# Layer 1 of a two-layer decoder trunk: spacing of the side tasks between the matmuls of the main stream

## The chip, the cores and the metric

The kernel runs on one core of one Trainium2 chip. A core has five engines with a queue each, which run at the same time and wait for one another by semaphores: PE (TensorE, matrix products, written to PSUM), DVE (VectorE, elementwise work), ACT (ScalarE, functions of one operand, copies and rounding), POOL (GpSimd, elementwise work), and SP (SyncE, which here only issues DMAs). Each engine takes its instructions strictly in the order of the program. The metric is the device time of one execution in microseconds (us).

## The reference

Input is x (512 tokens by 2048 channels) and a condition c. There are two layers, each an RMS norm with scale and shift from c, a branch, a SiLU gate and a gated residual add. Layer 0 is attention with 32 heads of 64. Layer 1, which the change is about, is RWKV-7 time mixing:

```python
xx = shift(h) - h                       # token shift
xr, xw, xk, xv, xa, xg = (h + xx * mu[i] for i in range(6))
r, k, v, z = xr @ w_in[0], xk @ w_in[1], xv @ w_in[2], xg @ w_in[3]
decay = exp(-exp(-softplus(-(w0 + tanh(xw @ w1) @ w2)) - 0.5))
v = v + (v_first - v) * sigmoid(v0 + (xv @ v1) @ v2)
a = sigmoid(a0 + (xa @ a1) @ a2)
kk = normalised(k * k_k);  k = k * (1 + (a - 1) * k_a)
# per head, state S (64 x 64), for every token in turn:
S = S * w_t + (S @ -kk_t) outer (kk_t * a_t) + v_t outer k_t
y_t = S @ r_t
# layer norm of y per head, bonus (r . k * r_k) v, then (y * silu(z)) @ w_out
```

Every product of the wide projections is computed as three single-pass products of a high and a low part (`hi*whi + hi*wlo + lo*whi`), so each weight and each operand is split into two parts first.

## The kernel before, in words

The activations lie with channels on the 128 partitions and the 512 tokens in the free dimension, so a 2048-channel operand is 16 tiles `[128, 512]`. A projection to 128 output channels is one bank of PSUM (`pj`) into which 16 x 3 = 48 matmuls of 128x512 accumulate. These matmuls form the **main stream** (`backbone`): in layer 1 ten tiles of k (six more are computed with the norm), then 16 each of r, v, z and the output projection. For each four k-steps a weight block is loaded (`raw`, three buffers), rounded by ACT (`whi`) and completed by DVE (`wlo = raw - whi`).

All else of layer 1 is written as **side tasks**, Python generators that record their instructions between the matmuls of the main stream. The order of every engine's queue is the order of recording; nothing is reordered afterwards. A planner, the class `Flow`, decides when a task goes on. It has a time `fl.t`, which each recorded matmul advances by its length at one column per 1/2400 us, so by 0.213 for a 128x512 matmul and 0.64 for a k-step of three. A task that yields d is resumed once `fl.t` has advanced by d. A number behind a `yield` is thus an amount of PE work that is put between two steps of a task, and nothing else; no wait is in it, and the semaphores still decide when an instruction runs.

The side tasks of layer 1, in order of time:

- `lora_k`, one for each of the 16 channel tiles, 4.4 apart: the token-shift mixes of three operands (`m`), their rounding (`mh`, on ACT) and rests (`ml`), and 9 matmuls into three banks (`S`, `S`, `y`). The rest of the first operand is made by POOL, those of the other two by DVE.
- `lora_up`, 48 of them: 2 or 3 matmuls each and a sigmoid on ACT (`sig`), loop in `side`.
- `keys`, one per channel tile, `KEY` apart: norms, decays and the matrices `at`, `bk`, `gab` of the recurrence. It has a call of `means`: ACT rounds a tile (`mhi`), DVE makes the rest (`mlo`), and PE multiplies both by a block matrix for a mean over each head.
- `invert` and `inverse`: inverses of small triangular matrices by 30 steps of two elementwise operations (`lt`, `lane`) for each of four groups, on POOL for the first three, on DVE for the last (`DG`), where `DINV` is the planner time over which they are spread. `inverse` comes `INV` after its keys.
- `stage`: for each of 16 pairs of chunks (a chunk is 64 tokens of 8 heads) the loads `rt`, `bk`, `prk`, and for each chunk `L`, `QP`, `SV`, two halves of each; then `products` and `bonus`.
- `recur`: 32 chunks in turn, three **hops** each. A hop is a group of small matmuls that needs what DVE copied out of PSUM after the hop before (`xs`, `SV`); `hop()` holds it until `fl.t` enters the next multiple of `HOP`. After each pair `normed` does the layer norm, with two calls of `means`; a token `B` keeps `bonus` and `normed` from using `means` together.
- `gated` and `output`: the gate, and the last projection.

SP's queue carries all loads and stores of both, in the recorded order.

Of the kernel before, what the change touches and what calls it, by code (L numbers as in the profile page):

```python
# [131 lines left out]
def body(ctx, tc, a, out, dbg=None, stop=0):  # L132
# [260 lines left out]
    with ExitStack() as s0:  # L393
# [7 lines left out]
        with tc.tile_pool(name="st0", bufs=2, reuse_waits="tile") as q:  # L401
# [96 lines left out]
            cb, cs, i = silu_c(cbp)  # L498
# [11 lines left out]
            for i in range(4):  # L510
                o = bank("tr")
# [79 lines left out]
        fl = Flow()  # L591
# [5 lines left out]
        q = sq0.enter_context(tc.tile_pool(name="at", bufs=2, reuse_waits="tile"))  # L597
# [445 lines left out]
    fl = Flow()  # L1043
# [7 lines left out]
    q = pools.enter_context(tc.tile_pool(name="kq", bufs=2, reuse_waits="tile"))  # L1051
# [36 lines left out]
    def means(q, w, x, th, tl):  # L1088
        hi = q.tile([P, T], R, tag=th, name="mhi")
        lo = q.tile([P, T], R, tag=tl, name="mlo")  # L1090
        act_hi(hi, x)
        yield 0.6
        dve.tensor_tensor(out=lo, in0=x, in1=hi, op=OP.subtract)
        yield 1.8
        n = yield from need("S")
        ss = bank("S")
        pe.matmul(ss, w, hi, start=True, stop=False)
        pe.matmul(ss, w, lo, start=False, stop=True)
        return ss, n
# [34 lines left out]
    lspan = ((0, LW), (LW, LW + LA_), (NL - P, NL))  # L1134
    lb, la = [], []

    def lora_k(q, k):
        if k == 0:
            lb.extend(bank(t) for t in "SSy")
        hp = load(mq, h1d[k], "hp", (P, T + 1), bufs=NHP)  # L1140
        raw = load(q, a["lora"][k], "rawl", (P, NL))
        yield 4
        wh = q.tile([P, 1, NL], R, tag="whl", name="whl")
        wl = q.tile([P, 1, NL], R, tag="wll", name="wll")
        act_hi(wh[:, 0], raw)
        ns = (1, 4, 3)
        ms = [q.tile([P, T], F, tag=f"m{n}", name="m", bufs=1 + (n == 3)) for n in ns]
        d = q.tile([P, T], F, tag="d", name="d")
        pool.tensor_tensor(out=d, in0=hp[:, 0:T], in1=hp[:, 1:], op=OP.subtract)
        ts = [tuple(q.tile([P, T], R, tag=f"m{x}{n}", name="m" + x) for x in "hl") for n in ns]  # L1150
        yield 1.4
        for i in range(5):
            if i == 1:
                dve.tensor_tensor(out=wl[:, 0], in0=raw, in1=wh[:, 0], op=OP.subtract)
            if i < 3:
                dve.scalar_tensor_tensor(out=ms[i], in0=d,
                                         scalar=vecs[:, V_MU + ns[i], k:k + 1],
                                         in1=hp[:, 1:], op0=OP.mult, op1=OP.add)
            if 1 <= i < 4:
                act_hi(ts[i - 1][0], ms[i - 1])  # L1160
            if 2 <= i:
                e = pool if i - 2 < 1 else dve
                e.tensor_tensor(out=ts[i - 2][1], in0=ms[i - 2], in1=ts[i - 2][0],
                                op=OP.subtract)
            yield 0.7
        yield 1
        sp.dma_start(mxd[0, k], ms[2])
        premixed.add((0, k))
        for t, o, (m0, m1) in zip(ts, lb, lspan):
            mm3(o[0:m1 - m0, :], (wh, wl), 0, t, k == 0, k == KT - 1, m0, m1)  # L1170
            yield 1
        if k == KT - 1:
            lb.append(None)
# [294 lines left out]
    def stage(q, g, u):  # L1468

        rt = q.tile([P, NJ, UC, C], F, tag="rt", name="rt", bufs=2)  # L1470
        sp.dma_start(rt.rearrange("p j c t -> p j (c t)"), rTd[g][:, u])
        bk = q.tile([P, NJ, UC, 2, C], F, tag="bk", name="bk", bufs=2)
        yield 1
        for i in range(2):
            for h in range(2):
                sp.dma_start(bk.rearrange("p j c i t -> p (j c) i t")[HS[h], :, i, :],
                             bkd[g][HS[h], u, i ^ h].rearrange("p j (c t) -> p (j c) t", c=UC))
            yield 0.6
        yield from take("prk")
        prk = q.tile([P, NJ, UC, C], F, tag="prk", name="prk", bufs=2)  # L1480
        sp.dma_start(prk.rearrange("p j c t -> p j (c t)"), ipd[g][:, u])
        yield STW
        eI = q.tile([P, NJ, UC, C], F, tag="eI", name="eI", bufs=2)
        act.activation(eI, prk, AF.Exp, scale=-EDEC)
        yield 1
        dec = q.tile([P, NJ, UC], F, tag="dec", name="dec", bufs=3)
        pool.tensor_copy(dec, eI[:, :, :, C - 1])
        dve.tensor_tensor(out=rt, in0=rt, in1=eI, op=OP.mult)
        yield 1
        for j in range(NJ):  # L1490
            for h in range(2):
                s = HS[h]
                dve.scalar_tensor_tensor(out=prk[s, j], in0=rt[s, j],
                                         scalar=vecs[s, V_RK, NJ * g + j:NJ * g + j + 1],
                                         in1=bk[s, j, :, 1 - h, :], op0=OP.mult, op1=OP.mult)
            yield 0.6
        while any(NJ * g + i not in vd for i in range(NJ)):
            yield 0.2
        for c in range(UC):
            yield from take("chunk")  # L1500
            m = NCH * g + UC * u + c
            L, SV = ([q.tile([P, NJ] + w, F, tag=f"{m}{h}", name=f"{m}{h}", bufs=4)
                      for h in range(2)] for m, w in (("L", [2, C]), ("SV", [C])))
            svs[m] = SV
            qp = QP[m % 4]
            for h in range(2):
                s, t = HS[h], OS[h]
                sp.dma_start(L[h][s, :, 0, :], atd[g][s, u, :, c * C:c * C + C])
                dve.tensor_copy(L[h][s, :, 1, :], rt[s, :, c])
                sp.dma_start(qp[h][s], qtd[NJ * g:NJ * g + NJ, 64 * c:64 * c + 64,  # L1510
                                           4 * h + u, :].rearrange("j p t -> p j t"))
                sp.dma_start(SV[h][t], vtd[g][(UC * u + c) * C:(UC * u + c + 1) * C, h])
                if u == c == 0:
                    pool.memset(SV[h][s], 0.0)
                yield 0.6
            fl.start(fl.t + STW, products(q, m, c, L, SV, qp, bk, eI, dec))
            yield 2
        fl.start(fl.t + 2, bonus(q, g, u, prk))

    def products(q, m, c, L, SV, qp, bk, eI, dec):  # L1520
# [55 lines left out]
    def hop():  # L1576
        n = fl.t // HOP
        while fl.t // HOP == n:
# [163 lines left out]


    STW = 5
    DG, DINV = (3,), 25
    HOP = 3.9
    INV, KEY = 54, 9.8

    def side(q):
        for j, o in enumerate(ks):  # L1750
# [8 lines left out]
        q = pools.enter_context(tc.tile_pool(name="uq", bufs=2, reuse_waits="tile"))  # L1759
# [8 lines left out]
        for j in range(KT):  # L1768
            for n in range(3):
                if j % 4 == 0 and j < KT - 4:  # L1770
                    fl.start(fl.t, lora_w(q, j // 4 + 1, n))
                fl.start(fl.t, lora_up(q, j, n))
                yield 0.8
        while len(ups) < 3 * KT:
            yield 0.2
        yield 3
# [75 lines left out]
```

## Time and profile before

| | |
|---|---|
| median of 3 runs | 2428.52 us (2423.59 to 2431.46) |
| the profiled execution, its own time | 2426.4 us |
| its span, first to last instruction | 2424.7 us |
| PE busy | 2312.1 us (95%), 13626 matmuls |
| DVE / ACT / POOL busy | 1607.0 / 1254.5 / 701.4 us |
| mean granted clock of PE | 0.984 |

The stages of layer 1 in the trace, in us from the start of the span: `lora_k` 1203 to 1297, `lora_up` to 1355, `keys` to 1606, the inversion on DVE to 1646, the last inverses to 1695, first staging to 1750, recurrence to 2190, and the rest of the main stream to the end.

How to read it: all recording goes through one helper, so each row says L90, and the names of the tiles (out<-in) tell the places apart. In a list of waits a row reads: engine and output, what it waited for, microseconds in total, number of waits, the longest. `PEclk` is the clock of PE that was granted, as a share of full speed. PE's matmuls overlap in the records, so the start-to-start distance tells its pace, not the duration of one.

### The profile page before, as it was taken

How to read it: one execution, taken by the hardware profiler on the slowest of the kernel's cores; microseconds unless marked ns; L12 is line 12 of the kernel's file. 1: busy time of each engine (PE TensorE's matmuls, PEld its weight loads, DVE VectorE, ACT ScalarE, POOL GpSimd, SP SyncE). 2: the span in 40 equal slices, each digit the busy share in tenths (PEclk: the TensorE clock that was granted, in tenths of full speed). 3: DMA queues.
4: the chain of work that ended last, by engine and by line, in shares of the span. 5: the costliest groups of instructions: out<-in, count | busy, mean ns of one | idle time of the engine just before them, and what ended most of it. 6: DMA issues, size and time to landing. Idle time of an engine off the chain costs nothing. (4 is left out here: it accounts for less than half of the span.)

```text
span 2424.7 us, 39355 instructions
## 1 busy us (share of the span) xinstructions
PE 2312.1 (95%) x13626; PEld 1806.3 (74%) x13626; DVE 1607.0 (66%) x2850; ACT 1254.5 (52%) x2298; POOL 701.4 (29%) x1114
## 2 busy tenths in 40 slices
PE   6998999999999999998999999989899989999999
PEld 4786677878777778886766766777677767777887
DVE  6887878788788545336797667675477777655322
ACT  4425655555555544225646777754354556665221
POOL 0002424434323110110141218851264445440000
PEclk8999999999999999999999999999999999999999
DMA  8865566666665265445756999877776776635443
GB/s 303 327 230 183 184 197 209 203 207 219 199 210 183 88 201 185 146 135 153 230 169 210 296 283 264 262 220 204 206 197 178 194 187 190 180 121 178 153 139 95
DMA packets 388150, 480.20 MB, mean 198 GB/s; under 512 B 146032, under 2 KB 217840, under 8 KB 384112
## 3 DMA queue, kind: packets, MB, share of 16 engines
q1 hardware_dynamic: 386288, 475.08, 63.5%
q0 software_dynamic: 1664, 2.63, 0.3%
q8 instruction: 107, 1.75, 0.3%
q14 instruction: 91, 0.75, 0.1%
HBM read 381.63 MB, written 95.95 MB: 197 GB/s over the span
## 5 line engine op out<-in xcount | busy, mean ns | idle before, releaser
L90 PE MATMUL pj<-hi,whi 128*128 128x512 f32 x2416 | 986.6, 408 | 11.9 <-ACT hi L90 8.2
L90 PE MATMUL pj<-hi,wlo 128*128 128x512 f32 x2416 | 958.9, 397 | 5.9 <-DVE wlo L90 5.9
L90 PE MATMUL pj<-lo,whi 128*128 128x512 f32 x2416 | 959.8, 397 | 0.0
L90 DVE TENSOR_TENSOR wlo<-raw,whi 128x512 fp32r<-128x512 f32 (+2 forms) x628 | 474.4, 762 | 281.7 <-ACT whi L90 279.3
L90 ACT ACTIVATE whi<-raw 128x512 fp32r<-128x512 f32 (+2 forms) x628 | 394.2, 634 | 418.7 <-PE pj L90 220.1
L90 PEld LDWEIGHTS pj<-hi,whi 128*128 128x128 f32 x2416 | 459.2, 190 | 117.2 <-ACT hi L90 9.0
L90 PEld LDWEIGHTS pj<-lo,whi 128*128 128x128 f32 x2416 | 458.0, 190 | 108.9 <-DVE lo L90 0.6
L90 PEld LDWEIGHTS pj<-hi,wlo 128*128 128x128 f32 x2416 | 459.6, 190 | 100.4 <-DVE wlo L90 7.4
L90 DVE CUSTOM_DVE_ANT_0 wm<-wm,cb 128x1024 f32<-128x1024 f32 x128 | 157.6, 1231 | 0.3
L90 POOL TENSOR_SCALAR SV<-SV,dec 64x64 f32<-64x64 f32 x224 | 98.3, 461 | 113.5 <-DVE SV L90 71.5
L90 ACT ACTIVATE pr<-Sm,mx 128x128 f32<-128x128 f32 (+3 forms) x128 | 71.6, 559 | 89.2 <-POOL mx L90 89.0
L90 POOL TENSOR_SCALAR mx<-mx 128x1 f32<-128x1 f32 x128 | 66.3, 518 | 160.4 <-DVE mx L90 111.3
L90 POOL TENSOR_SCALAR pr<-pr,rc 128x128 f32<-128x128 f32 (+3 forms) x128 | 94.8, 741 | 28.4 <-DVE rc L90 20.1
L90 DVE CUSTOM_DVE_ANT_0 Sm<-S,cmask 128x128 f32<-128x128 f32 (+3 forms) x128 | 62.0, 485 | 36.9 <-PE S L90 36.1
L90 POOL TENSOR_TENSOR lt<-lane 128x30 f32<-128x30 f32 (+14 forms) x90 | 62.4, 693 | 65.1 <-DMA lane<-mld 58.3
L90 POOL TENSOR_TENSOR lane<-lane,lt 128x30 f32<-128x30 f32 (+14 forms) x90 | 65.1, 723 | 7.1
L90 POOL TENSOR_TENSOR bk<-bk,eI 128x512 f32<-128x512 f32 x32 | 36.4, 1137 | 105.9 <-PE S L90 90.1
L90 PE MATMUL S<-k,q 128*128 128x128 f32 (+7 forms) x256 | 62.5, 325 | 0.0
L90 POOL TENSOR_TENSOR acc<-acc,sq 128x512 f32<-128x512 f32 x14 | 18.1, 1295 | 150.7 <-ACT sq L90 150.7
L90 PE MATMUL tr<-ident,pr 128*128 128x128 f32 x320 | 56.8, 276 | 4.4 <-DVE rc L90 1.6
L90 PEld LDWEIGHTS tr<-ident,pr 128*128 128x128 f32 x320 | 41.4, 141 | 25.1 <-ACT pT L90 7.6
L90 DVE SCALAR_TENSOR_TENSOR hp<-pj,gate,hp 128x512 f32<-128x512 f32 x16 | 12.0, 751 | 68.8 <-PE pj L90 68.8
(325 smaller groups left out, 3280.4 us busy)
## 6 DMA issues: line engine op xcount, KB each, us to landing
wm<-in_wmodT SPq DMA_DIRECT2D x132, 512.0 KB, 4.2
raw<-in_wz SPq DMA_DIRECT2D x128, 256.0 KB, 3.8
raw<-in_wo SPq DMA_DIRECT2D x128, 256.0 KB, 3.5
raw<-in_wv SPq DMA_DIRECT2D x124, 256.0 KB, 3.8
wm<-in_wmodT SPq DMA_DIRECT2D x30, 1024.0 KB, 7.1
raw<-in_wk SPq DMA_DIRECT2D x96, 256.0 KB, 3.6
raw<-in_wr SPq DMA_DIRECT2D x64, 256.0 KB, 4.6
raw<-in_wq SPq DMA_DIRECT2D x56, 256.0 KB, 3.5
```

The source lines that it names most:

```text
L90: self.last = f(*a, **k)
```

## The change

Six numbers and one order. In `means` the two yields grow by 0.6 each. In `lora_k` the yield ahead of the matmuls is 1.4 in place of 1, and the three operands are used in the order second, third, first. In `stage` the yields behind each pair of `bk` loads and behind each half of a chunk's loads grow, and the two behind them shrink. The inversion on DVE is spread over 32 in place of 25, `HOP` is 3.5 in place of 3.9, `INV` 56 in place of 54, `KEY` 10.6 in place of 9.8, and the steps of `lora_up` are 0.95 apart in place of 0.8.

```diff
 def means(q, w, x, th, tl):
         act_hi(hi, x)
-        yield 0.6
+        yield 1.2
         dve.tensor_tensor(out=lo, in0=x, in1=hi, op=OP.subtract)
-        yield 1.8
+        yield 2.4
 ...
 def lora_k(q, k):
-        yield 1
+        yield 1.4
         sp.dma_start(mxd[0, k], ms[2])
         premixed.add((0, k))
-        for t, o, (m0, m1) in zip(ts, lb, lspan):
+        for t, o, (m0, m1) in ((ts[i], lb[i], lspan[i]) for i in (1, 2, 0)):
             mm3(o[0:m1 - m0, :], (wh, wl), 0, t, k == 0, k == KT - 1, m0, m1)
             yield 1
 ...
 def stage(q, g, u):
                              bkd[g][HS[h], u, i ^ h].rearrange("p j (c t) -> p (j c) t", c=UC))
-            yield 0.6
+            yield 1.2
 ...
-                yield 0.6
-            fl.start(fl.t + STW, products(q, m, c, L, SV, qp, bk, eI, dec))
-            yield 2
+                yield 1.4
+            fl.start(fl.t + STW - 1, products(q, m, c, L, SV, qp, bk, eI, dec))
+            yield 1
 ...
     STW = 5
-    DG, DINV = (3,), 25
-    HOP = 3.9
-    INV, KEY = 54, 9.8
+    DG, DINV = (3,), 32
+    HOP = 3.5
+    INV, KEY = 56, 10.6
 ...
                 fl.start(fl.t, lora_up(q, j, n))
-                yield 0.8
+                yield 0.95
```

No instruction is added or taken away: the built programs hold the same 11325 matmuls (13626 in the profile, which has most of those on full float32 operands twice), and the same operations on DVE, ACT and POOL, in another order. Three places show what moves.

PE, in a `lora_k` step (`mh` and `ml` are the two parts of a mixed operand, `whl` and `wll` of its weights; `S`, `S`, `y` the banks of the first, second and third). Before:

```order
L90 MATMUL S<-mh,whl 96x512
L90 MATMUL S<-mh,wll 96x512
L90 MATMUL S<-ml,whl 96x512
L90 MATMUL pj<-hi,whi 128x512
L90 MATMUL pj<-hi,wlo 128x512
L90 MATMUL pj<-lo,whi 128x512
L90 MATMUL S<-mh,whl 96x512
L90 MATMUL S<-mh,wll 96x512
L90 MATMUL S<-ml,whl 96x512
```

and now:

```order
L90 MATMUL S<-mh,whl 96x512
L90 MATMUL S<-mh,wll 96x512
L90 MATMUL S<-ml,whl 96x512
L90 MATMUL pj<-hi,whi 128x512
L90 MATMUL pj<-hi,wlo 128x512
L90 MATMUL pj<-lo,whi 128x512
L90 MATMUL y<-mh,whl 128x512
L90 MATMUL y<-mh,wll 128x512
L90 MATMUL y<-ml,whl 128x512
```

The group that opens a step was the one with POOL's rest; now it is the second operand's, the third's (`y`) follows, and POOL's comes last of the three.

DVE, around the fourth `mlo` of the keys (`kk`, `at`, `bk` belong to the key ahead). Before:

```order
L90 TENSOR_TENSOR kk<-kk,aa 128x512
L90 TENSOR_TENSOR bk<-kk,eN 128x512
L90 TENSOR_TENSOR kk<-aa,kt 128x512
L90 TENSOR_TENSOR bk<-kk,eN 128x512
L90 TENSOR_TENSOR mlo<-sq,mhi 128x512
L90 TENSOR_TENSOR wlo<-raw,whi 128x512
L90 SCALAR_TENSOR_TENSOR m<-hp,vecs,m 128x512
L90 TENSOR_TENSOR wlo<-raw,whi 128x512
```

and now:

```order
L90 TENSOR_TENSOR kk<-kk,aa 128x512
L90 TENSOR_TENSOR bk<-kk,eN 128x512
L90 TENSOR_TENSOR wlo<-raw,whi 128x512
L90 TENSOR_TENSOR kk<-aa,kt 128x512
L90 TENSOR_TENSOR bk<-kk,eN 128x512
L90 TENSOR_TENSOR mlo<-sq,mhi 128x512
L90 SCALAR_TENSOR_TENSOR m<-hp,vecs,m 128x512
L90 TENSOR_TENSOR wlo<-raw,whi 128x512 x2
```

One more `wlo` of the main stream stands ahead of `mlo`, and more of the main stream between two keys: from the first to the last of the 16 `mhi` products PE has 660 `pj` matmuls where it had 606.

SP, the loads of two chunks in the staging (`L`, `QP`, `SV`, 64 KB each; `raw` is a weight block of the main stream). Before:

```order
L90 DMA L_17731<-atd 64x4x64
L90 DMA QP_17034<-qtd 64x4x64
L90 DMA SV_17733<-vtd 64x256
L90 DMA raw<-in_wv 128x512
L90 DMA L_17732<-atd 64x4x64
L90 DMA QP_17035<-qtd 64x4x64
L90 DMA SV_17734<-vtd 64x256
L90 DMA L_17787<-atd 64x4x64
L90 DMA QP_17042<-qtd 64x4x64
L90 DMA SV_17789<-vtd 64x256
```

and now:

```order
L90 DMA L_18008<-atd 64x4x64
L90 DMA QP_17218<-qtd 64x4x64
L90 DMA vtd<-vt 128x4x64 x2
L90 DMA SV_18010<-vtd 64x256
L90 DMA raw<-in_wv 128x512
L90 DMA L_18009<-atd 64x4x64
L90 DMA QP_17219<-qtd 64x4x64
L90 DMA SV_18011<-vtd 64x256
L90 DMA raw<-in_wv 128x512
L90 DMA L_18069<-atd 64x4x64
L90 DMA QP_17226<-qtd 64x4x64
L90 DMA SV_18071<-vtd 64x256
```

Weight blocks now stand between the halves more often. In PE's order the first chunk of the recurrence comes after 5340 `pj` matmuls (5247 before), the last after 6306 (6267 before), out of 7248; the last product of `means` after 6378 (6333), and the output projection begins after 6480 in both.

## The prediction

> **What bounds the kernel now.** I read the summary first, then layer 1 cut into its stages, then what PE waited for in each stage.
>
> ```profile
> PE 2312.1 (95%) x13626; PEld 1806.3 (74%) x13626; DVE 1607.0 (66%) x2850; ACT 1254.5 (52%) x2298; POOL 701.4 (29%) x1114
> core 0: us, PE busy (x) PEld busy (x) DVE busy (x) ACT busy (x) POOL busy (x), PEclk, DMA share, GB/s
> 1203.00:1297.00 94.00, 86.91 (x352) 60.70 (x351) 91.64 (x112) 46.01 (x87) 42.85 (x32) 1.00 0.53 166
> 1297.00:1355.00 58.00, 53.81 (x219) 41.17 (x218) 33.66 (x39) 46.64 (x77) 1.76 (x6) 0.97 0.86 275
> 1355.00:1606.00 251.00, 229.47 (x1508) 175.88 (x1506) 169.55 (x215) 181.03 (x334) 146.29 (x201) 0.97 0.91 266
> 1606.00:1646.00 40.00, 32.61 (x240) 25.43 (x239) 34.13 (x80) 14.52 (x26) 8.04 (x8) 0.91 0.72 217
> 1695.00:1750.00 55.00, 48.06 (x230) 37.42 (x231) 26.22 (x50) 16.72 (x30) 15.53 (x37) 0.94 0.78 213
> 1750.00:2190.00 440.00, 422.35 (x4216) 331.57 (x4212) 309.79 (x660) 246.80 (x428) 209.75 (x386) 0.99 0.65 178
> 2250.00:2300.00 50.00, 50.00 (x216) 40.24 (x215) 16.13 (x24) 11.39 (x18) 0.00 (x0) 1.00 0.46 143
> ```
>
> PE bounds the program: after the recurrence it runs dense, 216 matmuls in 50 us, 0.231 us each, to the end. No matmul is added or removed, so the time can change only by what PE loses in the stages between: its waits, and the share of the clock that was not granted (PEclk below 1.00). A planner unit of dense matmuls takes 0.231 / 0.213 = 1.08 us on the chip. One stage differs: in the first row, of `lora_k`, DVE is busy 91.64 of 94 us.
>
> **The change part by part.** *`lora_k`, its order and its later matmuls.* What PE waited for there (us in total, number, longest), and one step of DVE and POOL in order of time:
>
> ```profile
> PE S L90 <- POOL ml L90: 5.6, 12, 0.8
> PE S L90 <- DVE ml L90: 1.1, 6, 0.2
> ...
> 1248.64 0.74 DVE L90 SCALAR_TENSOR_TENSOR m<-d,vecs,hp 128x512 f32<-128x512 f32 x1
> 1249.64 2.43 DVE L90 SCALAR_TENSOR_TENSOR m<-d,vecs,hp 128x512 f32<-128x512 f32 x2
> ...
> 1250.12 1.39 POOL L90 TENSOR_TENSOR ml<-m,mh 128x512 fp32r<-128x512 f32 x1 [2.55 <-ACT mh L90]
> ```
>
> POOL's rest was used 3.1 planner units after it was recorded, and will be used after 5.5, so the 5.6 us of waits for it should go. The rests of DVE lose cover: 3.4 to 2.8 units, and 3.7 to 3.1, that is 0.65 us each. And DVE has 94 - 91.64 = 2.4 us to spare in the whole stage for an unchanged list of operations, so PE, let through earlier at POOL's operand, meets DVE's a little later. Ends: -6.7 us (all these waits go) and +10 us (16 steps of 0.65 us more). I take -1, nearest to DVE's 2.4 us of idle time.
>
> The same rows say why moving POOL's use cannot relieve DVE. One `m` takes 0.74 us; of the two that follow, the second ran while POOL subtracted (1250.12 to 1251.51), and the pair took 2.43. [...]
>
> *`lora_up`, 0.95 apart.* The order puts 69 `pj` matmuls between the first and the last of its products, in place of 39: 30 x 0.231 = 6.9 us more cover. PE's waits for it:
>
> ```profile
> PE x L90 <- ACT sig L90: 2.6, 2, 1.9
> PE S L90 <- ACT sig L90: 0.8, 2, 0.6
> ```
>
> With the clock, 0.03 x 58 = 1.7 us, 5.1 us are there to be had; I take -3 (ends -5.1 and 0, since ACT with 46.64 of 58 us can still be late).
>
> *`means` and `KEY` in the keys.*
>
> ```profile
> PE S L90 <- DVE mlo L90: 9.0, 11, 1.8
> PE S L90 <- ACT mhi L90: 6.1, 6, 2.1
> PE S L90 <- ACT gab L90: 2.9, 2, 1.6
> ```
>
> These are 18.0 us of the keys' 251. The product of `mhi` comes 1.2 units later after `mhi` is recorded, 1.3 us on the chip, and so does that of `mlo` (which itself is recorded 0.6 later). Seventeen waits of 15.1 us in total average 0.9, the longest are 1.8 and 2.1; with 1.3 us taken from each, only the tops of the longest stay. `KEY` adds 54 matmuls over 15 distances, 0.83 us for each key, in which ACT (181.03 of 251 us) and DVE clear their queues. What queues behind a later `mlo` on DVE is an `m` or `wlo`, and the weight blocks are prepared four ahead. I take 14 of the 18.0. Then the clock:
>
> ```profile
> 1438.51 0.50 PE L90 MATMUL S<-mhi,blkr 128*128 128x512 f32 x1 [0.77 <-ACT mhi L90]
> 1440.04 0.50 PE L90 MATMUL S<-mlo,blkr 128*128 128x512 f32 x1 [1.03 <-DVE mlo L90]
> 1440.38 0.41 PE L90 MATMUL pj<-hi,whi 128*128 128x512 f32 x1
> 1440.61 0.60 PE L90 MATMUL pj<-hi,wlo 128*128 128x512 f32 x1
> 1441.01 0.63 PE L90 MATMUL pj<-lo,whi 128*128 128x512 f32 x1
> 1441.43 0.63 PE L90 MATMUL pj<-hi,whi 128*128 128x512 f32 x1
> ```
>
> Two waits of 0.77 and 1.03 us, and right after them matmuls start 0.40 to 0.42 us apart in place of 0.23: the granted clock fell. It is 0.97 over the stage, 0.03 x 251 = 7.5 us; with the waits most of these falls go, and I take 5. Term: -19 (ends -25.5 and 0).
>
> [...]
>
> *The inversion on DVE over 32 units.*
>
> ```profile
> PE pj L90 <- DVE wlo L90: 4.8, 2, 3.7
> PE x L90 <- DVE t L90: 2.6, 4, 1.3
> ```
>
> DVE is busy 34.13 of these 40 us and falls behind the main stream. The same 60 operations over 7 units more leave 7.5 us for the rest. In play are 7.4 us of waits and 0.09 x 40 = 3.6 of clock; I take -7 (ends -11 and 0).
>
> *The staging, spread.* Between 1646 and 1750 the two rows that matter, PE's longest wait and what held ACT:
>
> ```profile
> PE S L90 <- ACT vt L90: 3.8, 1, 3.8
> ...
> ACT whi L90 <- DMA raw<-in_wv: 29.2, 13, 5.9
> ```
>
> A weight block that lands late holds ACT; a copy out of PSUM queued behind it (`vt`) holds a bank, and PE. More `raw` loads stand between the staging loads now. With the clock's 0.06 x 55 = 3.3 us, 7.1 are in play, but this is one meeting of two queues, which a new order can move as well as remove: -2 (ends -7.1 and 0).
>
> *The recurrence.* Its list of PE's waits, and one hop: its matmuls, DVE's copy, the next hop.
>
> ```profile
> PE S L90 <- DVE mlo L90: 4.2, 4, 1.6
> ...
> PE x L90 <- DVE xs L90: 1.0, 1, 1.0
> ...
> PE y L90 <- DVE SV L90: 0.7, 1, 0.7
> ...
> 2050.02 0.69 PE L90 MATMUL x<-SV,L 128*64 128x64 f32 x16
> ...
> 2051.20 0.42 DVE L90 COPY xs<-x 128x256 f32<-128x256 f32 x1
> ...
> 2053.84 0.69 PE L90 MATMUL x<-xs,QP 128*64 128x64 f32 x16
> ```
>
> The copy ended at 2051.62 and was used at 2053.84: 2.2 us to spare of 3.8. `HOP` takes at most 0.4 x 1.08 = 0.43 us from each of 96. By the order, it takes less: 966 `pj` matmuls lie in the recurrence in place of 1020, 54 x 0.231 = 12.5 us, 0.13 a hop, because the spread staging now sets the pace (its yields for a pair of chunks sum to 20.4 units of the 21 that six hops leave). Ends: 0 and 96 x 0.43 = 41 us, were every hop just in time. Only 2 of 96 waited, 1.7 us together; I take that once more, +2. The later `means` should halve the 4.2 us: -2. Term: 0.
>
> *The end.* The recurrence begins 93 `pj` matmuls later and ends 39 later. From the last `means` to the output projection are 102 matmuls in place of 147, 23.6 us in place of 34.0, in which the last norm is stored, loaded, gated and split. That costs nothing while it fits; each us beyond is a us of PE.
>
> **Sum.** -1 - 3 - 19 - 7 - 2 + 0 + 0 = -32 us. The profiled execution's own time is 2426.4 us (span 2424.7), so 2394.4; the median of the runs is 2428.5, 2.1 above that execution, so I predict 2396 us as the median.
>
> **The rivals.**
>
> - *The waits move on.* Each later step also shifts what follows, and DVE and ACT have the same work. For it speaks that the waits of the recurrence and the staging are meetings of queues; against it, that the keys get 54 matmuls of real cover. Half of the gain stays: 2412.
> - *The clock is not to be had.* [...] As a mechanism of this kernel: its falls are met elsewhere and stay, so 9 us of my terms (1 + 5 + 2 + 1) fall away: 2405. The rows at 1438 to 1441 speak against it.
> - *More than the sum.* The wider keys free the DMA engines (share 0.91), weight blocks land sooner, and all 25.5 us of the keys, the 11 of the inversion and the 5.1 of `lora_up` go: 2384.
> - *No net change.* The later `means` is met by a later DVE, the hops pay for the rest: 2427.
> - *Slower: the hops.* If DVE's queue in the denser recurrence (309.79 of 440 us before) takes up the 2.2 us to spare, each hop waits for its copy. From 32 / 96 = 0.33 us a hop on it eats the gain; at the full 0.43 us, 41 us, it is 9 us slower: 2437. The 2.2 us in the row speak against it.
>
> **How the numbers follow.** Chances: the sum 0.50 (2384 to 2408 by its own ends), waits move on 0.15, the clock 0.04, more than the sum 0.09, no net change 0.12, the hops 0.10. A measurement of this kernel can tell about 0.3%, 7 us, from no change. Faster by more: 0.50 + 0.15 + 0.04 + 0.09 = 0.78; within: 0.12; slower: 0.10. The range leaves out the slower case and the far half of the better one: 2380 to 2424.
>
> **What would show it.** In the keys, waits of PE for `mlo` and `mhi` under 5 us together and PEclk at 0.99: right; over 10: wrong. In `lora_k`, waits for POOL's `ml` gone and waits for DVE's in their place, with the stage still about 94 us long: right; a stage shorter by 5 us: DVE did not bound it. In the inversion, waits for `wlo` under 2 us. In the recurrence, waits for `xs` and `SV` under 5 us; over 20 makes the hop the cause. If PE waits for `hi` or `lo` of the gated operands in the output projection, the 23.6 us at the end were too few. What would make the prediction wrong as a whole is a new wait of several us, many times over, at a place not named here.

## The result, and the profile after

The changed kernel takes 2443.86 us (median of 5 runs, 2440.6 to 2446.87) against 2431.46 for the kernel before on the same chip: a ratio of 1.0058, 95% interval 1.0044 to 1.0073. It is slower by 12 us, where 32 us faster was forecast. The profiled execution has 2446.64 us, with a span of 2444.9.

To see where the time went, the trace is cut at the same places of the work in both kernels: first `lora_k` product, last one, end of `lora_up`, last `bk` row of the keys, last inverse, first and last product of the recurrence, end. These are the windows of the `pj` matmuls alone, of the kernel before (columns: window and its length, busy time and count of the `pj` matmuls, PEclk, DMA share, GB/s):

```profile
1203.10:1296.50 93.40, 55.02 (x205) 1.00 0.53 166
1296.50:1353.90 57.40, 22.50 (x87) 0.97 0.86 273
1353.90:1594.70 240.80, 182.60 (x732) 0.97 0.91 268
1594.70:1693.20 98.50, 78.91 (x312) 0.97 0.73 212
1693.20:1749.60 56.40, 43.31 (x168) 0.94 0.77 209
1749.60:2188.50 438.90, 267.61 (x1020) 0.99 0.65 177
2188.50:2424.70 236.20, 229.94 (x981) 1.00 0.47 143
```

and of the changed one:

```profile
1207.00:1302.30 95.30, 55.07 (x205) 1.00 0.54 171
1302.30:1363.40 61.10, 31.04 (x117) 1.00 0.86 274
1363.40:1631.20 267.80, 201.52 (x789) 0.94 0.86 250
1631.20:1734.10 102.90, 81.17 (x321) 0.95 0.74 215
1734.10:1782.70 48.60, 41.11 (x162) 0.93 0.81 210
1782.70:2213.80 431.10, 257.37 (x967) 0.99 0.64 175
2213.80:2444.90 231.10, 221.18 (x942) 1.00 0.45 140
```

A stage that holds more of the main stream is longer for that alone. So its **net loss** is its length minus that of before, less 0.231 us for each `pj` matmul that it has more. For the keys that is 267.80 - 240.80 - 57 x 0.231 = +13.8 us. Beside it stands what the prediction had:

| stage | net, us | predicted |
|---|---|---|
| ahead of `lora_k` (same work in both) | +3.9 | 0 |
| `lora_k` | +1.9 | -1 |
| `lora_up` | -3.2 | -3 |
| keys | +13.8 | -19 |
| inversion and last inverses | +2.3 | -7 |
| first staging | -6.4 | -2 |
| recurrence | +4.4 | 0 |
| to the end | +3.9 | 0 |

The first line has the same work in every kernel of this study. It lies between -0.2 and +5.5 in their profiled executions, so a single net number is good to some 3 us at best. The recurrence scatters more: six kernels with the same number of matmuls in it (after, a3, b1, b2, c1 and c3 below) have -0.3 to +10.7 there. The two profiled executions lie 20 us apart, the medians 12. Of the 52 us between the forecast (-32) and this execution (+20), 33 are in the keys. PE's waits there:

```profile
PE S L90 <- ACT gab L90: 10.2, 3, 5.4
PE x L90 <- DVE t L90: 8.5, 10, 3.1
PE S L90 <- DVE mlo L90: 4.5, 4, 2.4
...
PE S L90 <- ACT mhi L90: 0.7, 1, 0.7
```

The waits for `mlo` and `mhi` fell from 15.1 to 5.2 us, close to the forecast, but the later yields are not what did it, as a1 and a2 below show. The waits of the stage did not: they rose from 21.4 to 29.9 us, fewer and longer, with ACT's `gab` (2.9 before, 10.2 now) ahead. SP's and ACT's own waits tell more. Before:

```profile
SPq L90 <- DVE kk L90: 10.4, 13, 1.9
...
ACT whi L90 <- DMA raw<-in_wr: 28.2, 20, 3.3
```

and after:

```profile
SPq L90 <- DVE kk L90: 31.0, 18, 4.4
...
ACT whi L90 <- DMA raw<-in_wr: 43.0, 25, 6.3
```

One such meeting in the changed kernel, in order of time (start, duration, operation, idle time before it and its releaser; SP rows are DMA issues):

```profile
1447.31 0.58 SPq L90 DMA_DIRECT2D ip<-ipd  x1
1451.32 0.34 SPq L90 DMA_DIRECT2D kt<-kTd  x1
...
1452.67 0.42 SPq L90 DMA_DIRECT2D raw<-in_wr  x1
...
1458.75 0.43 SPq L90 DMA_DIRECT2D raw<-in_wr  x1
...
1450.60 0.69 DVE L90 TENSOR_TENSOR kk<-aa,kt 128x512 f32<-128x512 f32 x1 [0.56 <-ACT aa L90]
...
1464.33 0.63 ACT L90 ACTIVATE whi<-raw 128x512 fp32r<-128x512 f32 x1 [3.57 <-DMA raw<-in_wr]
...
1469.48 1.56 ACT L90 ACTIVATE gab<-S 64x256 f32<-64x256 f32 x4
...
1470.29 0.80 PE L90 MATMUL S<-mhi,blkr 128*128 128x512 f32 x1 [4.16 <-ACT gab L90]
```

The load of `kt` for the key after the next writes one of two buffers. Its last reader, `kk<-aa,kt` of an earlier key, now runs later, since its key waited longer inside `means`. SP stands from 1447.89 to 1451.32 (that reader ended at 1451.29), and all that is recorded behind it stands too: stores, weight blocks; from there its issues follow one another up to the weight block at 1458.75 and beyond. ACT then stands 3.57 us at a `whi` whose block has not landed, eight further operations of ACT come ahead of the `gab` that frees a bank, and PE stands 4.16 us for the bank. This is one meeting, read link by link; a3 below asks which of the links carries the loss.

### The profile page after: what moved, and what is told of

Read it like the earlier page. It is cut to its first block, busy times and chain, and to the rows that moved or that the text cites. A ratio compares the mean times of both kernels' runs of the same rounds, so it can differ in the third digit from the quotient of the medians.

```text
span 2444.9 us, 39350 instructions
## 1 busy us (share of the span) xinstructions
PE 2314.0 (95%) x13626; PEld 1812.7 (74%) x13626; DVE 1601.7 (66%) x2850; ACT 1254.1 (51%) x2298; POOL 695.7 (28%) x1114
## 3 DMA queue, kind: packets, MB, share of 16 engines
q8 instruction: 108, 1.77, 0.3%
## 5 line engine op out<-in xcount | busy, mean ns | idle before, releaser
L90 PE MATMUL pj<-hi,whi 128*128 128x512 f32 x2416 | 989.5, 410 | 13.2 <-ACT hi L90 8.2
```

Source lines behind the costliest of these rows:

```text
L90: self.last = f(*a, **k)
```

## The experiments

The runs were compared with the kernel before on the same chip each time. "Net" is as above, from the one profiled execution; the verdicts go by the ratios. "Short means" are the yields 0.6 and 1.8 of the kernel before.

| run | edit | median, us | ratio (95%) |
|---|---|---|---|
| | the changed kernel | 2443.9 | 1.0058 (1.0044 to 1.0073) |
| a1_means_undone | short means | 2421.9 | 0.9974 (0.9960 to 0.9989) |
| a2_means_alone | before + long means | 2439.3 | 1.0029 (1.0019 to 1.0038) |
| a3_loads_later | keys' loads later | 2437.8 | 1.0031 (1.0018 to 1.0043) |
| a4_hop_undone | HOP 3.9 | 2455.5 | 1.0098 (1.0083 to 1.0113) |
| b1_norm_into_bv | `dc` free earlier | 2442.1 | 1.0062 (1.0040 to 1.0084) |
| b2_both_freed | a3 and b1 | 2430.9 | 1.0014 (1.0001 to 1.0026) |
| b3_key_undone | a1, KEY 9.8, INV 54 | 2438.4 | 1.0036 (1.0011 to 1.0062) |
| b4_lora_undone | `lora_k` as before | 2451.1 | 1.0096 (1.0072 to 1.0120) |
| c1_keys_short | short means in keys | 2438.0 | 1.0043 (1.0027 to 1.0059) |
| c2_norm_short | short means elsewhere | 2432.7 | 1.0025 (1.0011 to 1.0039) |
| c3_lane_later | inversion starts later | 2448.2 | 1.0087 (1.0071 to 1.0102) |
| c4_short_later | a1 and a3 | 2420.8 | 0.9967 (0.9952 to 0.9982) |
| d1_dinv_undone | a1, DINV 25 | 2428.8 | 0.9999 (0.9989 to 1.0009) |
| d2_lora_alone | before + `lora_k` new | 2434.9 | 1.0021 (1.0007 to 1.0035) |
| d3_key_hop_alone | before + KEY, INV, HOP | 2453.8 | 1.0105 (1.0085 to 1.0125) |
| d4_short_later_bv | c4 and b1 | 2419.2 | 0.9968 (0.9953 to 0.9982) |
| e1_stage_undone | a1, staging as before | 2439.0 | 1.0039 (1.0026 to 1.0052) |
| e2_hop_alone | before + HOP 3.5 | 2447.3 | 1.0067 (1.0049 to 1.0084) |

**The means: undone, and alone.** The theory: the longer chain of a key, by the later means, is the loss. The rival: the means are harmless and another of the six numbers is.

```diff
 a1: the changed kernel          a2: the kernel before
-        yield 1.2               -        yield 0.6
+        yield 0.6               +        yield 1.2
 ...                              ...
-        yield 2.4               -        yield 1.8
+        yield 1.8               +        yield 2.4
```

> The changed kernel with the two yields of means back at 0.6 and 1.8, all else as changed. Theory (the later means stretch a key's chain by 1.2 units and the norm's by 2.4, so tiles with one or two buffers come free later, and SP and ACT, which reuse them, stand still and hold up weight blocks): SP's waits for kk in the keys fall from 31 us to about 10, ACT's wait for ys on the store of dc from over 10 us to few, PE loses 12 us less there and pays some 8 us of waits for mlo again; about 2435 us, 8 to 12 under the changed kernel. Rival (the moved spacing of keys and hops, KEY 10.6 and HOP 3.5, makes the long stalls, whatever means does): 2443 or more, since the waits for mlo come back on top.

> The kernel before with the two yields of means at 1.2 and 2.4 and nothing else. Theory (stretched chain): with keys only 9.8 apart the reuse of kt and aa comes even sooner after the last reader, so SP's waits for kk rise from 10 us to over 30, and the time is 2440 or more, 10 us above the kernel before. Rival (spacing is to blame, later means are good by themselves): 2410 to 2420, as the waits of PE for mlo and mhi in the keys, 15 us, go.

Undone, the time falls by 22 us (20 by the ratios) and beats the kernel before; alone, it rises by some 7. In the changed kernel the later means are therefore more than the whole loss. In the keys, net by stage, a2 stands at +15.2 and a1 at +3.5; SP's wait for `kk` is 25.3 us in a2. In a1:

```profile
SPq L90 <- DVE kk L90: 12.3, 14, 2.1
```

The two runs also tell what cut PE's waits for `mlo` and `mhi`. In the keys, in a2 and then in a1:

```profile
PE S L90 <- DVE mlo L90: 8.7, 6, 2.7
PE S L90 <- ACT mhi L90: 5.5, 2, 3.1
...
PE S L90 <- DVE mlo L90: 4.8, 5, 1.8
PE S L90 <- ACT mhi L90: 3.5, 3, 2.1
```

With the long means as the only edit 14.2 of the 15.1 us stay, in fewer and longer waits. With short means and the wider keys 8.3 are left. Over all runs the two waits come to 14.2 to 20.4 us where `KEY` is 9.8, and to 5.2 to 11.7 where it is 10.6, with means of either length. The wider keys cut these waits; the longer yields by themselves hardly did so.

**The link by SP's queue.** If the loads of `kt` and `aa` stop SP, recording them later, with the same total of yields, must take the loss away without touching the means.

```diff
 def keys(q, j):
         sp.dma_start(u3(ip), of(ipd, j))
+        yield 3
         kt = load(q, kTd[j], "kt", bufs=2)
         aa = load(q, aad[j], "aa", bufs=2)
-        yield 8
+        yield 5
```

> The changed kernel, in which a key's loads of kt and aa are recorded 3 units after that of ip, so 3 units later, and are still used 5 units after; same work. Theory (SP stands at the reuse of kt and aa and holds the weight blocks behind): SP's waits for kk fall from 31 us to under 8, ACT's for in_wr in the keys from 43 to about 28, the three long waits of PE there (4 to 6 us each) go with 10 us of clock, 2430 us. Rival (the weight blocks are late because the DMA engines are busy, share 0.86 to 0.91): waits for in_wr and the time stay, 2443.

The wait of SP nearly goes:

```profile
SPq L90 <- DVE kk L90: 2.9, 8, 0.7
```

and the keys fall from +13.8 to +4.1 net, with the long means still in; b2 below, with the same edit, has +4.5. So SP's stand at these two loads cost the stage about 9 us. The links behind SP are not shown by it. I had expected ACT's wait for weight blocks to fall to about 28 us and PE's long waits to go, and a3 has in the keys

```profile
ACT whi L90 <- DMA raw<-in_wr: 36.6, 17, 6.0
...
PE S L90 <- ACT gab L90: 11.1, 6, 6.8
```

All waits of PE in the stage fall from 29.9 to 26.4 us only, while PEclk goes from 0.94 to 0.96. And in a2 ACT waited 24.5 us for weight blocks, less than the 28.2 before the change, in a stage with +15.2. The time as a whole falls by less, 6 us, as the recurrence of this run stands at +8.3 in place of +4.4.

**Which call of means.** Three places call it: `keys`, `bonus`, and `normed` twice.

```diff
-    def means(q, w, x, th, tl):
+    def means(q, w, x, th, tl, d=0):
         act_hi(hi, x)
-        yield 1.2
+        yield 1.2 - d
         dve.tensor_tensor(out=lo, in0=x, in1=hi, op=OP.subtract)
-        yield 2.4
+        yield 2.4 - d
 ...
 c1: d = 0.6 in the call in keys; c2: d = 0.6 in the calls in bonus and normed
```

> The changed kernel, with the two yields of means back to 0.6 and 1.8 in its call in keys alone; bonus and normed keep 1.2 and 2.4. If the longer chain of a key is what the change lost by, nearly all of what taking both back gave (22 us) comes with this call: 2422 to 2428, the waits of the keys' loads for kk near 12 us in place of 31. If it was the calls in the recurrence, or a new phase of the stages behind, it stays at 2438 to 2444.

> The counterpart: the changed kernel with 0.6 and 1.8 in bonus and normed, and 1.2 and 2.4 in keys. If the keys' chain is the cause, 2438 to 2444 and the keys' loads still wait for kk some 31 us. If the recurrence is the cause, 2422 to 2430. Both runs of this pair near 2432 would mean that each call has half of it.

c1 came out at the edge of its second end, c2 between its two. The keys alone back to short give -4 us by the ratios, which the two intervals cannot tell from nothing; the others back give -8; both give -20. The part outside the keys is thus no smaller. By stages it is sharper, as several runs share an order of work in a stage:

| | net in the keys | net from the recurrence to the end |
|---|---|---|
| long means there | +11.1 to +15.2 (after, a2, a4, b1, b4, c2, c3) | +3.8 to +14.0 with HOP 3.5 (after, a3, b1, b2, c1, c3) |
| short means there | +0.1 to +3.9 (a1, c1, d1, e1) | -0.7 to +3.1 (a1, c2, c4, d4) |
| long, loads later | +4.1, +4.5 (a3, b2) | |
| short, loads later | -3.0, -2.8 (c4, d4) | |

So the long means cost about 11 us in the keys (means of 13.1 and 1.9). With the loads later 7 of them are left (4.3 and -2.9), so SP's stand is only a part of what the long means do there. What is left goes with PE's wait for `gab`, 11.1 and 11.5 us in a3 and b2 against 2.4 and 1.5 in c4 and d4; why ACT is late with it stays open.

Behind the keys the difference is about 9 us (9.8 and 1.2), but the six runs with long means share one order of the recurrence and the four with short means another. Runs with other orders are not in that column: b4 with long means has +15.1, and with short means b3 has +7.2 and d1 +8.1 (and e1, with the staging as before, +11.4). So the 9 us are the difference of two orders; that the longer yields cost as much in any order is not shown. In the kernel before, with hops of 3.9, they cost nothing in the recurrence (a2: -4.2 from its start to the end).

**Inside the recurrence.** There PE waited for `tok`, and ACT for a buffer that the norm's store still read:

```profile
PE S L90 <- ACT tok L90: 10.6, 3, 5.3
PE S L90 <- DVE mlo L90: 5.8, 6, 2.3
...
ACT ys L90 <- DMA ypd<-dc: 17.4, 5, 5.5
```

With the norm's result written over `bv`, `dc` (which shares its one buffer with `ys`) is free without that store:

```diff
-            dve.scalar_tensor_tensor(out=dc[:, s], in0=dc[:, s], scalar=col(V_LB, NJ * g + j),
+            dve.scalar_tensor_tensor(out=bv[:, s], in0=dc[:, s], scalar=col(V_LB, NJ * g + j),
                                      in1=bv[:, s], op0=OP.add, op1=OP.add)
-        free["bv"] += 1
         yield 1.8
-        sp.dma_start(ypd[g][:, u], dc.rearrange("p (j t) -> p j t", j=NJ))
+        sp.dma_start(ypd[g][:, u], bv.rearrange("p (j t) -> p j t", j=NJ))
+        free["bv"] += 1
```

> The changed kernel, in which the norm's last four operations write their result over bv, from where it is stored, so that the tile dc (one buffer, shared with ys) comes free with DVE's last read and not with the landing of the store; same work. Theory: ACT stands 17.4 us in the recurrence at ys, waiting for the store of dc (5 waits, the longest 5.5), and two of them make PE's waits of some 5 us for tok; these waits on the store go, PE's waits for tok fall from 10.6 to under 4 us, with some 5 us of clock; 2434 to 2438. Rival (the copies behind ys are late for another reason, the shorter hop or the staging): 2443.

> The changed kernel with the norm's result over bv and with the later loads of kt and aa, both late-freed tiles relieved at once, the long yields of means kept. Theory: the two gains add, 6 and 6 to 9 us, 2428 to 2432, which brings it to the kernel before, but not to the 2422 of the changed kernel with short yields if the long yields gain nothing by themselves. If the later means are worth something once no tile is late: under 2422. Rival (another cause): above 2437.

ACT's waits for that store are gone in b1, and PE's list there now reads:

```profile
PE S L90 <- DVE mlo L90: 6.4, 7, 2.3
PE S L90 <- ACT tok L90: 4.3, 3, 3.1
PE S L90 <- DVE vf L90: 3.9, 3, 1.5
PE S L90 <- DVE bv L90: 2.1, 2, 1.6
```

The time is the same: what `tok` lost, others gained. The store now holds `bv`, and PE's waits for `bv` (0.7 to 2.1 us) and `vf` (1.0 to 3.9) rose. This part of the theory fell. With the keys' loads later as well (b2) it is 11 us faster than the changed kernel by the ratios, 4 of them beyond a3, which lies within the two intervals. What the long means hold up inside the recurrence is thus not settled. Of their 9 us there, about 4 lie after it, and those are shown next.

**The end.** After the last `means`, its norm is stored, loaded, gated and split under the `pj` matmuls that are left ahead of the output projection: 147 before, 102 in the changed kernel, 129 in a1, and 24 with the old hop.

```diff
-    HOP = 3.5
+    HOP = 3.9
```

> The changed kernel with HOP back at 3.9. Theory: the recurrence loses 4.8 us and the stretch after it 4.3 us more than before because dc is stored late and the last norms come close to the output projection; a slower hop gives the norms time but ends the recurrence later still, so 2440 to 2446, no clear change. Rival (the shorter hop itself makes PE wait): 5 to 10 us less than the changed kernel, 2435.

What PE waited for from the end of the recurrence on, in the changed kernel and in a4:

```profile
PE pj L90 <- DVE wlo L90: 3.0, 3, 2.0
...
PE pj L90 <- ACT z L90: 13.8, 1, 13.8
```

Net to the end: +0.7 with 129 matmuls, +3.9 with 102, +14.9 with 24. All six runs with 102 matmuls have +3.3 to +5.4, all runs with 129 or more -1.0 to +0.8, so this reading is firm. Of the 27 matmuls between a1 and the changed kernel, 18 are a last hop that comes later and 9 a longer last norm. a4 is slower than both of its ends: the shorter hop is what pays for a recurrence that starts later.

**The wider keys.** a1 with the old distance:

```diff
-    INV, KEY = 56, 10.6
+    INV, KEY = 54, 9.8
```

> The changed kernel with the yields of means undone and KEY 9.8 and INV 54 as before: what is left of the change is lora_k, lora_up, the staging, DINV and HOP. Theory (the wider keys gain nothing by themselves, the keys lost 29.5 us before and 31.3 with KEY 10.6 and short means): 2420 to 2425, as with KEY 10.6. Rival (the wider keys are what makes the changed kernel with short means 9 us faster than the kernel before): 2431.

My theory had no gain from them. They are worth 15 us in this kernel (0.9974 to 1.0036, good to some 7 us). But the gain is not in the keys: there, net +6.3 with 9.8 and +3.5 with 10.6, less apart than the scatter. The recurrence has +7.3 against +2.4, the first staging -4.6 against -8.4. So with short means and 54 more matmuls the keys lose no less than before (+0.1 to +3.9): the cover that the prediction counted halved PE's waits for `mlo` and `mhi` (7.0 to 8.3 us in a1, c1, d1 and e1) and yet bought the stage nothing, at a PEclk of 0.94 to 0.95 in place of 0.97.

**Keys and hops alone, and the hop by itself.**

```diff
 d3: the kernel before           e2: the kernel before
-    HOP = 3.9                   -    HOP = 3.9
-    INV, KEY = 54, 9.8          +    HOP = 3.5
+    HOP = 3.5
+    INV, KEY = 56, 10.6
```

> The kernel before with KEY 10.6, INV 56 and HOP 3.5 as the only edits. If the wider keys give their 15 us by themselves and the shorter hops cost nothing, 2413 to 2420. If the denser recurrence (its chain takes 333 planner units in place of 362) pays for its hops as the slower rival had it, 2430 to 2445, with waits of PE for xs and SV of over 20 us.

> The kernel before with HOP 3.5 as the only edit; the chain takes 325 planner units in place of 362. If the shorter hops cost by themselves, 2440 to 2455, the recurrence losing some 20 us more than the 28 it loses before, by waits for mlo, bv and tok and not for xs and SV. If it was the wider keys that left a bad start, 2426 to 2432.

Both are slower, by 26 and 16 us. Net in the recurrence: +21.8 and +13.2. PE's waits there, in d3 and in e2:

```profile
PE S L90 <- DVE mlo L90: 11.1, 9, 3.1
PE S L90 <- DVE bv L90: 5.0, 4, 2.3
...
PE S L90 <- DVE mlo L90: 11.9, 8, 2.8
PE x L90 <- DVE SV L90: 4.9, 6, 1.7
PE S L90 <- ACT GP L90: 4.5, 5, 2.5
```

The waits for `xs` and `SV` that d3 was to show, over 20 us, came to 1.6. I read the rows as the same lists of DVE and ACT in a shorter recurrence: the side work is late, its banks and operands with it. In e2 also the hop's own copy (`SV`), which I had ruled out.

**The spread staging.** a1 with the yields of `stage` as before, which lets the recurrence run at the pace of the hops:

```diff
-            yield 1.2
+            yield 0.6
 ...
-                yield 1.4
-            fl.start(fl.t + STW - 1, products(q, m, c, L, SV, qp, bk, eI, dec))
-            yield 1
+                yield 0.6
+            fl.start(fl.t + STW, products(q, m, c, L, SV, qp, bk, eI, dec))
+            yield 2
```

> The changed kernel with the short means everywhere and the staging as before (0.6 and 0.6, then 2). Its recurrence is then denser: its chain takes 329 planner units in place of 347. Base is the run with the short means, 2421.9 us. If the spread staging is what keeps the shorter hops from costing, 2436 to 2450, with the loss in the recurrence, as in the run with keys and hops alone. If the denser recurrence costs nothing, 2418 to 2426.

It is 16 us slower than a1, with +12.3 net in the recurrence in place of +2.4, as in e2. Without the spread the three runs with a hop of 3.5 have +12.3 to +21.8 there, with it and short means six runs have -0.1 to +8.1. The spread is what keeps most of the cost of the shorter hops away.

**The inversion.** a1 with DINV 25, and the changed kernel with the inversion begun 7 units after its load, over 25 units, so that it ends at the same place:

```diff
 d1: a1                          c3: the changed kernel
-    DG, DINV = (3,), 32         -    DG, DINV = (3,), 32
+    DG, DINV = (3,), 25         +    DG, DINV = (3,), 25
                                 -    fl.t + (DINV + 8 if ...
                                 +    fl.t + (DINV + 15 if ...
                                  ... ahead of the first step, where grp in DG:
                                 +            yield 7
```

> The changed kernel with the short means (0.6 and 1.8) everywhere and the inversion on DVE over 25 units again. Base is the run with the short means, 2421.9 us. If the spread gives the 7 us that the prediction had for it, 2427 to 2431. If it gives nothing, 2420 to 2424. If it costs (the last inverses come 7 units later, and what follows with them), 2415 to 2419.

> The changed kernel; the inversion on DVE begins 7 planner units after its load is recorded and runs over 25 units in place of 32, so it ends where it ended. DVE then has no first step standing in its queue while the load of lane is on its way (one wait of 8.9 us). If that wait is what kept the term of the inversion from being gained, the stage loses about 6 us less and the time is near 2438. If the wait for lane costs PE nothing, or the steps packed closer cost as much, no change: 2442 to 2446.

The spread is worth 6 us (0.9974 to 0.9999), near the size forecast, and the stage has 4.9 of them (net +7.9 with 25, +3.0 with 32). But in the same two profiles the keys differ by 3.4 the other way and the stretch from the recurrence to the end by 5.0, so how much of the 6 us is the stage's own is not shown. PE still waited 8.3 us for `wlo` there in a1, and 10.7 in d1. In c3 DVE's 8.9 us at `lane` are gone and PE's waits for `wlo` fall from 7.5 to 3.4 us, but the stage has +2.0 in place of +2.3: that wait was not what kept the term from showing. As a whole c3 is 7 us slower by the ratios, with +7.8 in the recurrence, whose order it shares with the changed kernel (+4.4) and c1 (+10.7). The stage lost something else by its new place, which stays open.

**`lora_k`.** The old order and yield in the changed kernel (b4), and the new ones alone in the kernel before (d2):

```diff
 b4: the changed kernel
-        yield 1.4
+        yield 1
-        for t, o, (m0, m1) in ((ts[i], lb[i], lspan[i]) for i in (1, 2, 0)):
+        for t, o, (m0, m1) in zip(ts, lb, lspan):
 d2: the kernel before, the same lines the other way
```

> The changed kernel with lora_k as before, operands in the order first, second, third and the yield at 1. Theory (DVE bounds the stage, 92.84 of 95 us busy, and the waits only moved from POOL's operand to DVE's): within 3 us of the changed kernel, 2442 to 2446, PE's waits for DVE's ml gone and for POOL's back. Rival (POOL's operand was a real cost): 2449 or more.

> The kernel before, with the order second, third, first and the yield of 1.4 in lora_k as the only edit. If the predicted term (-1 us) holds and nothing behind it moves, 2426 to 2432, no change. If the order frees PE of the 5.6 us of waits for POOL, 2422 to 2425. If the new phase that it leaves decides what follows, any of 2420 to 2440, with the difference in stages behind lora_k.

The stage itself has +1.8 net in d2, +0.8 in b4, +1.9 in the changed kernel. Over all runs it has 1.5 on average with the new order and 0.8 with the old, so the new order gains nothing there and costs at most about 1 us. The waits moved as expected: in b4 those for POOL's `ml` are back (5.7 us) and those for DVE's are down to 1.9. Yet the runs differ by 9 us (b4, slower without it) and 5 us (d2, slower with it). So b4 has the time of its rival, but not for the rival's reason: it has +15.6 in the recurrence. An edit of `lora_k` shifts which matmul of the main stream every later task meets; I have no account of it finer than that, and a single such edit cannot be told from that shift.

**Both kernels beaten.** Short means with the keys' loads later, and that with the norm written over `bv`:

> The changed kernel with means back at 0.6 and 1.8 everywhere and the loads of kt and aa recorded 3 planner units after that of ip, the total of the yields unchanged. If SP's queue standing at these two loads is a cost of its own, both gains add: 2415 to 2420. If the long means were what made the loads late, the second edit finds nothing left to gain: 2420 to 2424. A new phase of what follows can move either by some us.

> The changed kernel with the short means, the loads of kt and aa 3 units later, and the norm's result written over bv, so that the buffer of dc is not held by its store. If the two costs add on top of the short means, 2411 to 2417. If the short means leave nothing to gain there, 2418 to 2424.

c4 has 0.9967 and d4 0.9968, against 0.9974 for a1: faster than both kernels, by some 8 us and 22 us, and not to be told from a1. In the keys the later loads do give some 5 us (+1.9 on average over a1, c1, d1 and e1, to -3.0 and -2.8), since SP still stood 12 us at `kk` with the short means. A third buffer for `kt` and `aa`, the more direct cure, was not tried.

## Why the prediction was wrong

**Where it failed: the keys' term, -19 us.** Two of its steps failed.

The first is the cover, "with 1.3 us taken from each, only the tops of the longest stay". By a2 the later yields alone leave 14.2 of the 15.1 us. The fall to 5.2 us in the changed kernel, which looks like the forecast, is mostly that of the wider keys, so there the number was met by luck. One size in that step was wrong from the start: the product of `mlo`, which has 9.0 of the 15.1 us, comes only 0.6 units later after `mlo` is recorded (2.4 for 1.8), not 1.2. And the step took a wait as lost time of its own: in a1, c1, d1 and e1 these waits are half of before, and the keys are no better.

The second is "what queues behind a later `mlo` on DVE is an `m` or `wlo`". I had looked for what is queued behind `mlo` and not for who waits for the end of the key. A key's chain is longer by two yields, its last reader frees `kt` and `aa` later, and SP stands at their loads (10.4 to 31.0 us). a1 and a2 show that the longer yields make the loss of the stage; a3 and b2 show that SP's stand has about 9 us of it. How that stand reaches PE, over late weight blocks and ACT's queue as in the meeting above, is argued and not shown, and the 7 us that the longer yields cost with the loads out of the way stay open.

The **clock** part of that term failed with it: PEclk went from 0.97 to 0.94 instead of to 0.99. It also was no sum of its own. In e2 the keys have the same order as before the change, and their window reads

```profile
1358.50:1600.40 241.90, 216.01 (x1406) 165.81 (x1404) 167.23 (x209) 175.44 (x321) 138.74 (x187) 0.99 0.92 267
```

PEclk 0.99 in place of 0.97, and yet 241.90 us in place of 240.80: PE was busy 3.3 us less (216.01 for 219.27) and waited 4.4 us longer (25.8 for 21.4). With most falls gone the stage was no shorter. This one pair of profiles, good to some 3 us, speaks against the 0.03 x 251 = 7.5 us as a gain on top of the waits; it does not settle it.

**The inversion, -7.** By d1 the spread is worth 6 us in the kernel with short means. But the stage of the changed kernel has +2.3, and PE's waits for `wlo` in it rose from 4.8 to 7.5 us where under 2 was forecast. c3 rules out the wait at `lane`; the cause stays open.

**The recurrence, 0.** The argument on the hops was right for the reason given, that the spread staging sets the pace: e1 and e2 show 10 and 13 us where it does not. The -2 for later `means` holds in a2, with the old hops: PE's waits for `mlo` there fell from 4.2 to 0.7 us. In the changed kernel it was wrong in sign: they rose to 5.8 us, and the stretch from the recurrence to the end costs about 9 us more in the order that came with the longer calls. **The end, 0**, failed in "that costs nothing while it fits": 102 matmuls did not quite fit, by about 4 us.

**Right, in part by luck:** `lora_up` has -3.2 for -3 in this profile, but over the fifteen kernels with its edit -0.4 to -3.3, on average -1.6. For `lora_k` the mechanism held, PE's waits moved from POOL's rests to DVE's, in the rows of the changed kernel

```profile
PE S L90 <- DVE ml L90: 7.9, 9, 1.6
...
1207.00:1302.30 95.30, 85.35 (x348) 60.55 (x348) 92.88 (x112) 46.12 (x86) 42.07 (x32) 1.00 0.54 171
```

with DVE 92.88 us busy of 95.30; it cost up to 2 us and did not gain 1. DVE was slower beside POOL's subtraction: of the 45 `m` that the trace of the kernel before has in this stage, the 8 that ran some 1.2 us beside POOL's `ml` took 1.76 to 1.78 us, and the other 37, at most 0.26 us beside it, 0.73 to 0.75; in the changed kernel 9 took 1.77 to 1.79 and 36 the shorter time. A DVE so busy would hold the stage without that as well, and no run here tells the two apart. The staging's -2 was -6.4 by stage; over all runs it is -7.9 on average with the spread and -2.9 without, so some 5 us are the edit's own. Its real use, holding the recurrence apart, is only a side remark in the prediction.

**The rivals.** "The waits move on" named the mechanism and set its price too low: half of the gain, where more than all of it went. "Slower: the hops" is what the hop does alone (e2), for a queue of DVE as it said, but not why this kernel is slower.

## What to carry to other kernels

A short and frequent wait of the bounding engine in a pipelined stage can be the place where a loop of buffers closes, as here, where SP's stand at `kt` and `aa` rose from 10.4 to 31.0 us and had about 9 us of the stage. Before giving it cover, follow the operand to its last reader and ask which load stands, at the head of which queue, until that reader is done. Spacing edits hold each other up: a longer step in a side task must be checked against the number of buffers it holds, the pace of the stage, and what is left ahead of the end. With edits of this kind the total alone does not tell them apart. Net loss by stage over several runs with the same order did so in the keys and at the end; in the recurrence, where each edit also changes the order, it did not.

## What the runs showed of the hardware

In the traces of the two kernels the granted clock is 1.00 or 0.50, all its falls and rises lie whole multiples of 3.41 us apart, and a fall went with how little PE was busy in the 3.41 us ahead of it, not with the length of one wait. The place that the prediction quoted, in the kernel before, and a longer one in the changed kernel, cut at the falls (columns: window, length, busy time of PE, PEld, DVE, ACT, POOL, PEclk, DMA share, GB/s):

```profile
1437.20:1440.60 3.40, 1.60 (x6) 0.77 (x5) 2.60 (x5) 3.01 (x7) 0.00 (x0) 1.00 0.78 195
1440.60:1444.00 3.40, 3.40 (x9) 2.28 (x7) 0.81 (x3) 3.14 (x5) 0.00 (x0) 0.50 0.96 305
1444.00:1447.40 3.40, 3.40 (x27) 2.78 (x26) 2.58 (x4) 2.01 (x5) 0.00 (x0) 0.99 0.94 278
...
1465.30:1468.70 3.40, 0.83 (x4) 0.36 (x2) 2.29 (x3) 3.38 (x7) 3.09 (x5) 1.00 0.37 114
1468.70:1475.50 6.80, 5.21 (x12) 4.13 (x13) 4.08 (x5) 4.93 (x10) 6.17 (x9) 0.50 0.92 269
```

A step with PE busy 1.60 of 3.40 us, after two waits of 0.77 and 1.03, was followed by one at half clock, and the next was at full again. The step from 1396.25 us in the kernel before, with PE busy 1.72 of 3.41 us and one longer wait of 1.69, was followed by one at full clock. Cutting both traces into such steps from 1200 us on: of those with PE busy under half, 10 of 10 (before) and 12 of 12 (after) were followed by half clock; of the others 2 of 347 and 6 of 350. Of these eight, three were at full clock and busy for 52 to 58%, and five were themselves steps at half clock. Of the 30 steps at half clock in the two traces, the 23 that were followed by a full one had PE busy for 80 to 100%, the 7 followed by another at half for 3 to 95%. At full clock 20 of 20 with PE busy under half were followed by half clock, and 3 of 669 over. By these steps I estimate that each one at half clock costs PE at most half of 3.41, 1.7 us, and less where PE waits anyway.
